# A decoder step on one core: side work issued behind the evictions of each product instead of in front of them

## The chip, the cores and the metric

The kernel runs on one core of one Trainium2 chip. The metric is the device time of one execution in microseconds (us), over three runs: median 2305.31, from 2304.89 to 2305.92. TensorE is called PE here, VectorE DVE, ScalarE ACT, GpSimd POOL; SP is the engine that issues most of the loads.

## The reference

A hybrid decoder of two layers (one of each kind), model width 2048, for 1024 prompt positions and 8 sampled positions. All is fp32.

```python
def pool_layer(x, prefix, pos, w_in, w_grp, scale, w_out, g_ln, b_ln):
    z = x @ w_in
    u, gate = z[..., :D_POOL], z[..., D_POOL:]
    d, new_state = multiscale_pool(u, prefix, pos)      # trailing means of 2, 4, 8, 16 minus u
    d = jnp.einsum('btgc,gce->btge', d.reshape(B, T, N_POOL_GROUPS, POOL_GROUP), w_grp)
    d = d.reshape(B, T, D_POOL) * scale
    y = (d * jax.nn.silu(gate)) @ w_out
    return layer_norm(ALPHA * x + y, g_ln, b_ln), new_state

def attn_layer(x, pos, kb, vb, k_pos, q_pos, blocked, w_in, sinks, w_out, g_ln, b_ln):
    z = x @ w_in
    q = rope_partial(z[..., :D_ATTN].reshape(B, T, N_HEADS, HEAD_DIM), pos)
    gate = z[..., D_ATTN:]
    o = attn_core(q, kb, vb, q_pos, k_pos, sinks)       # window of 128, grouped heads, sinks
    y = (o.reshape(B, T, D_ATTN) * jax.nn.silu(gate)) @ w_out
    return layer_norm(ALPHA * x + y, g_ln, b_ln)
```

Between the two layers one shared K and V is projected from the first layer's output. The outputs are both layers' result for prompt and sample, the pooling states and the last keys and values.

## The kernel before

**Tiles and chunks.** Activations lie with channels on the 128 partitions and positions along the free dimension. The 1032 positions are two chunks: chunk 0 with 512, chunk 1 with 520. Ten phases run one after another: `ai` (first layer's input product and pooling), `ao` (its output product), `bi` (K, V, queries, gates and the attention) and `bo` (output product), each for chunk 0 and then chunk 1; `ai0` and `bi0` are split in two.

**Products.** Almost all matrix products are Strassen-like: a pair of 128-column output tiles by 2x2 blocks takes seven products, in the order 0, 2, 1, 5, 3, 4, 6 (the function `seven`). One product is 24 matmuls (L661 to L663) into one of three PSUM banks: eight steps of high half by high half, high by low, low by high, since an fp32 operand is split in a high and a low half (fp32r) on the way. A product takes 24 times 120 ns, 2.88 us, and a pair some 20.2 us. In the first pairs of some phases two pairs run side by side.

**Weight casts.** A stream of weight blocks is loaded ahead, cast to its high half on ScalarE (L491), and the low half is the difference on VectorE (L506). `begin`, at the start of each product, issues the L506 of the product two later. The input's halves are cast likewise (L796 on ScalarE, L805 on VectorE) by `x_tick`, at the end of a product.

**Evictions.** Each product leaves a function in `self.posts`, which `flush`, called first by the next `begin`, issues: L609, L615, L618, L624 and L641 are copies on ScalarE after products 0, 1, 2, 5 and 6; L629 and L634 are subtractions on VectorE after products 3 and 4. Bank b takes products 0's negative, 1, 3 and 6, so L609, L618 and L629 must be done before the product after the next one. Behind the last eviction of a pair, in the same list, comes what is done with the pair: in `ao` and `bo` the residual addition L1287 on VectorE (ALPHA times x plus the pair, which reads what L641 copied); L1298 and L1301 add the pair to a running sum.

**Side work.** `self.side` is a list of generators, advanced by one step now and then (`self.every`) when enough slots are free: `t_gen` makes the Strassen sums of an activation (`t_ops`, L853 to L856), `sum_gen` those of a weight (L439, L443, L444, each followed by a store from POOL's queue), `ln_gen` is the norm: sums over the channels by matmuls with a constant matrix (L910), variance L1005, the reciprocal root L931 to L934, then for each of eight tile pairs minus the mean and times the root on VectorE (L1026, L1029), scale and offset on ScalarE (L1018), a store, and the next layer's sums (`t_ops`). The norm of chunk 0 runs beside the output product of chunk 1 (`ao1`, 925 to 1080 us, and `bo1`, from 2145 us); weight sums of `woa` run in `ai1`, the norm of chunk 1 in `bi0`. The sums of `wob` go through `self.extra`, which is not `self.side`.

**Order.** PE, VectorE and ScalarE run in the order of the source (`in_order` at the end makes it so). SP's and POOL's queues are ordered by the framework's scheduler. All SBUF tiles share 54 slots; a new tile gets the slot that was released longest ago, so the order of allocation decides which slot a tile lies in.

So at the border between two products the order before was: `end` of the product (events, `x_tick`, one step of side work), then `begin` of the next (`flush` with the evictions, loads, weight casts, matmuls).

Of the kernel before, what the change touches and what calls it, by code (L numbers as in the profile page):

```python
# [94 lines left out]
class Slot:  # L95


    def __init__(self, mem, i, h, a):
        self.mem, self.i, self.h, self.a = mem, i, h, a
# [83 lines left out]
class Kern:  # L183
    def __init__(self, ctx, tc, io):
        self.tc, self.io = tc, io
        self.nc = tc.nc
        pool = lambda name, **kw: ctx.enter_context(tc.tile_pool(name=name, **kw))
        one = pool("one", bufs=1)
        self.smp = pool("smp", bufs=2)
        dram = pool("dram", bufs=1, space=bass.MemoryType.DRAM)  # L190
        self.psd = [pool(f"psd{i}", bufs=1, space=bass.MemoryType.PSUM) for i in range(3)]
        self.pso = pool("pso", bufs=1, space=bass.MemoryType.PSUM)
        self.four = None
        ctx.callback(self.use_four, None)
        self.prm = one.tile([P, N_PRM], F32, name="prm")
        self.cst = one.tile([P, N_CST], F32, name="cst")
        self.mki = one.tile([P, 64], U8, name="mki")
        self.jr = one.tile([P, P], F32R, name="jr")
        area = one.tile([P, NK * NST], F32, name="area")
        three = lambda a, b, c: area[:, a : a + b * c].rearrange("p (b c) -> p b c", b=b)  # L200
        self.carry = three(0, NK, NST)
        self.kdec, self.qd, self.sgd = three(0, 2, NDEC), three(16, NDEC, 8), three(80, 8, NDEC)
        self.flag = one.tile([P, 1], F32, name="flag")
        self.mem = Mem(pool("mem", bufs=1), NSLOT)
        self.n = 0
        self.i = self.e = self.lastO = self.turns = self.ring = 0
        self.posts, self.events, self.side = [], {}, []
        self.extra, self.on = None, False
        self.fresh = None
        self.ahead = 7, 4, 3  # L210
        dr = lambda n, s: dram.tile(s, F32, tag=n, name=n)
        self.Td, self.act, self.l_sq, self.l_sh = {}, {}, {}, {}
        for c, (_, T) in enumerate(CHUNKS):
            for n, k in (("x", "ai"), ("g", "ao"), ("h", "bi"), ("o", "bo")):
                if (k, c) in STRASSEN:
                    self.Td[n, c] = dr(f"t{n}{c}", [P, 8, 4, T // 2])
            self.act["x", c] = io[f"x{c}"]
            for n in ("g", "h", "o", "p"):
                self.act[n, c] = dr(f"{n}{c}", [P, NK, T])
        self.gbd = dram.tile([32, 2 * P], F32, tag="gbd", name="gbd")  # L220
        self.ws = {
            n: [dr(f"s{n}{q}", [P, 4, 1024]) for q in range(np_)]
            for n, np_ in (("wia", 16), ("woa", 8), ("wkv", 2), ("wib", 16), ("wob", 8))
        }
# [288 lines left out]
    def flush(self):  # L513
        todo, self.posts = self.posts, []
        for go in todo:
            go()

    def begin(self):
        self.flush()
        a, b, d = self.ahead if self.strassen else (5, 4, 3)  # L520
        free = lambda: len(self.mem.whole())
        self.load_to(self.e + min(a, 5))
        while self.loaded < min(self.e + a, len(self.stream)) and free() > 2:
            self.load_to(self.loaded + 1)
        self.prep_to(self.e + (d if free() > 1 else d - 1))
        self.cast_to(self.e + (b if free() > 1 else b - 1))
        self.make_to(self.e + (b if free() > 0 else b - 1) + (1 if self.strassen else 0))
        self.e += 1
        return self.hl.pop(self.e - 1)

    def end(self):

        if self.late and self.i > 6:
            self.late.pop(0)()
        while self.i in self.pe:
            todo = sorted(self.pe.pop(self.i), key=lambda x: x[0])
            todo[0][1]()
            if todo[1:]:
                self.pe.setdefault(self.i, []).extend(todo[1:])
        for go in self.events.pop(self.i, []):  # L540
            go()
        self.i += 1
        self.x_tick()
        room = len(self.mem.whole()) - 2 * len(self.xq)
        if self.extra and next(self.extra, 1):
            self.extra = None
        if self.side and int(self.i / self.every) != int((self.i - 1) / self.every) and room >= self.room:
            if next(self.side[0], 1):
                self.side.pop(0)

    def side_step(self):
        if self.lastO >= self.i - 1:
# [706 lines left out]
    def phase_out(self, c, res, nxt, last=None):  # L1259
# [55 lines left out]
        return pre, acc  # L1315

    def shifted(self, c, p, s, pre, acc, end):

        nc = self.nc
# [1180 lines left out]
```

## Time and profile before

| | |
|---|---|
| runs shown | 2305.31 us (median of 3; 2304.89 to 2305.92) |
| profiled execution | 2305.89 us |
| its span, first to last instruction | 2304.1 us |
| granted PE clock | 0.999 of full speed |
| L506, low half of a weight, VectorE | 684 times, 1218 ns each |
| L491, high half of a weight, ScalarE | 684 times, 1048 ns each |
| L629, eviction on VectorE | 90 times, 423 ns each; VectorE idle ahead of it 74.9 us, for PE |
| L641, eviction on ScalarE | 87 times, 374 ns each; ScalarE idle ahead of it 188.5 us, for PE |
| DMA | 654.58 MB, mean 284 GB/s |

A timeline row has the start and the length in us, engine, line, operation, tile written from tiles read, shape, count, and in brackets the engine's idle time just before it and what ended that. Busy instructions of one engine overlap a little, so the next row can start before the last has ended. A PE row's length is that of a pipelined matmul; matmuls start every 0.12 us.

### The profile page before, as it was taken

To read this page: it belongs to the slowest core of one execution; us is meant where nothing else is said; L and a number is where in the kernel's file an instruction comes from. 1 tells how busy PE (TensorE), PEld (TensorE's weight loads), DVE (VectorE), ACT (ScalarE), POOL (GpSimd) and SP (SyncE) were. 2 spreads that over 40 slices of the span, in tenths; PEclk is the share of its full clock that TensorE was granted. 3 is DMA by queue.
4 is the path that set the end of the run, shared out by engine and by line. 5 is a ranking of instruction groups with operands and counts; after the bars stand their busy time and mean duration, and the time that the engine had idled before them with its cause. 6 is when DMAs were issued, how large, how long until landed. Compare 5 with 4: busy or idle time off the path is not lost. (4 is left out here: it accounts for less than half of the span.)

```text
span 2304.1 us, 50417 instructions
## 1 busy us (share of the span) xinstructions
PE 2283.5 (99%) x20279; PEld 2209.6 (96%) x20279; DVE 1902.1 (83%) x2433; ACT 1368.2 (59%) x2533; POOL 198.1 (9%) x400
## 2 busy tenths in 40 slices
PE   9999999999999999999999999999999999999998
PEld 7899999999999999999889999999999999999998
DVE  8787889777878878988888888899776777888896
ACT  4444446544546546555466776785776678656565
POOL 0111110011010000000011111100000000010001
PEclk9999999999999999999999999999999999999999
DMA  8768789988989988999687667787686678799794
GB/s 292 243 233 296 262 298 364 328 306 289 309 306 313 350 286 305 338 389 351 230 305 255 230 231 248 256 291 233 223 255 229 218 225 306 250 364 383 254 347 172
DMA packets 248220, 654.58 MB, mean 284 GB/s; under 512 B 26385, under 2 KB 106033, under 8 KB 247985
## 3 DMA queue, kind: packets, MB, share of 16 engines
q1 hardware_dynamic: 204816, 494.67, 63.8%
q0 software_dynamic: 43168, 156.68, 17.6%
q8 instruction: 159, 2.61, 0.5%
q14 instruction: 77, 0.62, 0.1%
HBM read 464.54 MB, written 177.20 MB: 279 GB/s over the span
## 5 line engine op out<-in xcount | busy, mean ns | idle before, releaser
L661 PE MATMUL pD<-m,m 128*128 128x260 f32 (+1 forms) x4976 | 1409.1, 283 | 6.8 <-DVE m L629 3.0
L662 PE MATMUL pD<-m,m 128*128 128x260 f32 (+1 forms) x4976 | 1401.8, 282 | 0.0
L663 PE MATMUL pD<-m,m 128*128 128x260 f32 (+1 forms) x4976 | 1401.2, 282 | 0.6 <-DVE m L506 0.5
L661 PEld LDWEIGHTS pD<-m,m 128*128 128x128 f32 x4976 | 936.8, 188 | 12.1 <-issue 2.3
L663 PEld LDWEIGHTS pD<-m,m 128*128 128x128 f32 x4976 | 937.3, 188 | 1.1 <-DVE m L506 1.1
L662 PEld LDWEIGHTS pD<-m,m 128*128 128x128 f32 x4976 | 936.8, 188 | 0.5
L506 DVE TENSOR_TENSOR m<-m,m 128x1024 fp32r<-128x1024 f32 x684 | 827.6, 1218 | 76.7 <-ACT m L491 42.9
L491 ACT CAST m<-m 128x1024 fp32r<-128x1024 f32 x684 | 712.8, 1048 | 286.8 <-DVE m L343 86.4
L343 DVE TENSOR_TENSOR m<-m,m 128x1024 f32<-128x1024 f32 x120 | 146.6, 1222 | 10.2 <-DMA m<-in_wia 6.9
L805 DVE TENSOR_TENSOR m<-m,m 128x1024 fp32r<-128x1024 f32 (+1 forms) x118 | 144.2, 1225 | 5.9 <-ACT m L796 3.2
L641 ACT COPY m<-pD 128x260 f32<-128x260 f32 (+1 forms) x87 | 32.5, 374 | 188.5 <-PE pD L663 188.5
L796 ACT CAST m<-m 128x1024 fp32r<-128x1024 f32 (+1 forms) x118 | 123.8, 1054 | 4.4 <-DMA m<-in_x 2.4
L689 PE MATMUL pD<-m,m 128*128 128x512 f32 x288 | 114.3, 397 | 0.0
L691 PE MATMUL pD<-m,m 128*128 128x512 f32 x288 | 113.5, 394 | 0.0
L690 PE MATMUL pD<-m,m 128*128 128x512 f32 x288 | 113.2, 393 | 0.0
L629 DVE TENSOR_TENSOR m<-pD,m 128x260 f32<-128x260 f32 (+1 forms) x90 | 38.1, 423 | 74.9 <-PE pD L663 74.9
L1870 ACT ACTIVATE m<-m,sm 128x128 f32<-128x128 f32 x256 | 99.3, 390 | 0.0
L1892 ACT ACTIVATE m<-m,sm 128x128 f32<-128x128 f32 (+1 forms) x320 | 93.8, 373 | 0.0
L1133 PE MATMUL pD<-m,m 128*128 128x260 f32 (+1 forms) x528 | 91.4, 323 | 0.0
L1133 PEld LDWEIGHTS pD<-m,m 128*128 128x128 f32 x528 | 79.4, 188 | 8.2
L618 ACT COPY m<-pD 128x260 f32<-128x260 f32 (+1 forms) x90 | 33.6, 374 | 90.3 <-PE pD L663 90.2
L609 ACT ACTIVATE pD<-pD 128x260 f32<-128x260 f32 (+1 forms) x88 | 32.5, 369 | 78.2 <-PE pD L663 68.2
(257 smaller groups left out, 2187.4 us busy)
## 6 DMA issues: line engine op xcount, KB each, us to landing
m<-in_wib SPq DMA_DIRECT2D x132, 512.0 KB
m<-in_wia SPq DMA_DIRECT2D x122, 512.0 KB
swia<-m POOLq DMA_DIRECT2D x64, 512.0 KB, 5.0
m<-swia SPq DMA_DIRECT2D x64, 512.0 KB
m<-swoa SPq DMA_DIRECT2D x64, 512.0 KB
m<-swob SPq DMA_DIRECT2D x56, 512.0 KB
m<-in_wob SPq DMA_DIRECT2D x52, 512.0 KB
m<-in_woa SPq DMA_DIRECT2D x48, 512.0 KB
```

What stands on the lines that cost most here:

```text
L343: self.nc.vector.tensor_add(s[out].a[:, :1024], s[x].a[:, :1024], s[y].a[:, :1024])
L491: self.nc.scalar.copy(hi.r[:, :1024], self.stream[self.cast].src().a[:, :1024])
L506: self.nc.vector.tensor_sub(lo.r[:, :1024], s.src().a[:, :1024], hi.a[:, :1024])
L661: nc.tensor.matmul(ps[:, :TH], wh[:, s], h, start=new and k == 0, stop=False, skip_group_check=on)
L662: nc.tensor.matmul(ps[:, :TH], wh[:, s], l, start=False, stop=False, skip_group_check=on)
L663: nc.tensor.matmul(ps[:, :TH], wl[:, s], h, start=False, stop=k == 7, skip_group_check=on)
L689: nc.tensor.matmul(ps[:], wh[:, s], h, start=par == 0 and k == 0, stop=False)
L690: nc.tensor.matmul(ps[:], wh[:, s], l, start=False, stop=False)
L691: nc.tensor.matmul(ps[:], wl[:, s], h, start=False, stop=par == 1 and k == 7)
L796: self.nc.scalar.copy(h.r[:, :n], s.a[:, :n])
L805: self.nc.vector.tensor_sub(l.r[:, :n], s.a[:, :n], h.a[:, :n])
L1133: nc.tensor.matmul(ps[:, : cs.stop - cs.start], ws[:, s], d[:, cs], start=f0 and k == 0, stop=l0 and k == 3,)
```

## The change

One step of side work that falls due in `end` is now only noted (`self.owed`), and `flush` issues it when it has issued the evictions. What else `end` does, `x_tick`'s input casts among it, stays where it was. A step that other code asks for directly (`side_step`) is issued at once, as before.

```diff
@@ Kern.__init__
-        self.posts, self.events, self.side = [], {}, []
+        self.posts, self.events, self.side, self.owed = [], {}, [], False
@@ flush
         todo, self.posts = self.posts, []
         for go in todo:
             go()
+        if self.owed and self.side:
+            self.owed = False
+            if next(self.side[0], 1):
+                self.side.pop(0)
@@ end
         if self.side and int(self.i / self.every) != int((self.i - 1) / self.every) and room >= self.room:
-            if next(self.side[0], 1):
-                self.side.pop(0)
+            self.owed = True
```

Three places show what moves. Lines behind `flush` are three or four higher in the changed kernel: L629, L634, L932, L1026, L1029, L1287 and L1301 before are L632, L637, L935, L1029, L1032, L1290 and L1304 after. Names m_.. are SBUF tiles, pD_.. PSUM banks.

VectorE in `ao1`, at 948 us, where the first full pair ends and the norm of chunk 0 has its mean and root (m_1304_10982). Before:

```order
L634 TENSOR_TENSOR m_1306_10986<-pD_10874,m_1312_11022 128x260
L506 TENSOR_TENSOR m_1343_11273<-m_1328_11135,m_1341_11244 128x1024
L1026 TENSOR_TENSOR m_1057_8981<-m_1057_8981,m_1304_10982 128x1024
L1029 TENSOR_TENSOR m_1057_8981<-m_1057_8981,m_1304_10982 128x1024
L1287 SCALAR_TENSOR_TENSOR m_1298_10945<-m_1279_10824,m_1298_10945 128x1040
L506 TENSOR_TENSOR m_1347_11310<-m_1331_11166,m_1344_11275 128x1024
```

And after:

```order
L637 TENSOR_TENSOR m_1304_10982<-pD_10874,m_1312_11022 128x260
L506 TENSOR_TENSOR m_1343_11273<-m_1328_11135,m_1341_11244 128x1024
L1290 SCALAR_TENSOR_TENSOR m_1298_10945<-m_1279_10824,m_1298_10945 128x1040
L1029 TENSOR_TENSOR m_1057_8981<-m_1057_8981,m_1305_10984 128x1024
L1032 TENSOR_TENSOR m_1057_8981<-m_1057_8981,m_1305_10984 128x1024
L506 TENSOR_TENSOR m_1347_11310<-m_1331_11166,m_1344_11275 128x1024
```

The norm's two steps have moved behind the residual addition; the weight cast stays last.

VectorE one pair later, at 970 us: the Strassen sums of a normed tile pair, the eviction of product 4, the norm of another tile pair and the residual addition. Before:

```order
L506 TENSOR_TENSOR m_1370_11521<-m_1353_11383,m_1368_11492 128x1024
L853 TENSOR_TENSOR m_1372_11549<-m_1057_8981 128x256
L854 TENSOR_TENSOR m_1372_11549<-m_1057_8981 128x256
L855 TENSOR_TENSOR m_1372_11549<-m_1057_8981,m_1372_11549 128x256
L856 TENSOR_TENSOR m_1372_11549<-m_1057_8981,m_1372_11549 128x256
L634 TENSOR_TENSOR m_1365_11486<-pD_11389,m_1357_11416 128x260
L506 TENSOR_TENSOR m_1374_11558<-m_1358_11418,m_1371_11523 128x1024
L1026 TENSOR_TENSOR m_1352_11373<-m_1352_11373,m_1304_10982 128x1024
L1029 TENSOR_TENSOR m_1352_11373<-m_1352_11373,m_1304_10982 128x1024
L1287 SCALAR_TENSOR_TENSOR m_1365_11486<-m_1356_11414,m_1365_11486 128x1040
L1301 TENSOR_TENSOR m_1278_10823<-m_1278_10823,m_1365_11486 128x1040
L506 TENSOR_TENSOR m_1379_11601<-m_1361_11449,m_1375_11560 128x1024
```

And after:

```order
L506 TENSOR_TENSOR m_1370_11521<-m_1353_11383,m_1368_11492 128x1024
L637 TENSOR_TENSOR m_1364_11479<-pD_11389,m_1357_11416 128x260
L856 TENSOR_TENSOR m_1372_11550<-m_1057_8981 128x256
L857 TENSOR_TENSOR m_1372_11550<-m_1057_8981 128x256
L858 TENSOR_TENSOR m_1372_11550<-m_1057_8981,m_1372_11550 128x256
L859 TENSOR_TENSOR m_1372_11550<-m_1057_8981,m_1372_11550 128x256
L506 TENSOR_TENSOR m_1374_11558<-m_1358_11418,m_1371_11523 128x1024
L1290 SCALAR_TENSOR_TENSOR m_1364_11479<-m_1356_11414,m_1364_11479 128x1040
L1304 TENSOR_TENSOR m_1278_10823<-m_1278_10823,m_1364_11479 128x1040
L1029 TENSOR_TENSOR m_1352_11376<-m_1352_11376,m_1305_10984 128x1024
L1032 TENSOR_TENSOR m_1352_11376<-m_1352_11376,m_1305_10984 128x1024
L506 TENSOR_TENSOR m_1379_11601<-m_1361_11449,m_1375_11560 128x1024
```

The four sums have moved behind the eviction, and the two steps of the norm behind the residual addition and the running sum.

VectorE in `bo1`, at 2174 us: the reciprocal root of the last norm of chunk 0 and the eviction of product 3. Before:

```order
L1341 TENSOR_TENSOR m_2786_26370<-m_2805_26489,m_2812_26527 128x1040
L932 TENSOR_TENSOR m_2868_26988<-m_2844_26793 128x512
L933 SCALAR_TENSOR_TENSOR m_2868_26988<-m_2868_26988 128x512
L934 SCALAR_TENSOR_TENSOR m_2844_26793<-m_2868_26988,m_2844_26793 128x512
L629 TENSOR_TENSOR m_2873_27028<-pD_26908,m_2863_26945 128x260
L506 TENSOR_TENSOR m_2878_27069<-m_2859_26911,m_2876_27034 128x1024
```

And after:

```order
L1344 TENSOR_TENSOR m_2786_26370<-m_2805_26489,m_2812_26527 128x1040
L632 TENSOR_TENSOR m_2874_27025<-pD_26903,m_2864_26946 128x260
L935 TENSOR_TENSOR m_2869_26990<-m_2844_26794 128x512
L936 SCALAR_TENSOR_TENSOR m_2869_26990<-m_2869_26990 128x512
L937 SCALAR_TENSOR_TENSOR m_2844_26794<-m_2869_26990,m_2844_26794 128x512
L506 TENSOR_TENSOR m_2879_27070<-m_2860_26912,m_2877_27035 128x1024
```

Here the eviction has moved ahead of the root's three steps.

## The prediction

> **What bounds the kernel now.** I read the page first, then the list of waits of TensorE (PE), then the busy times by stage, and last the timeline around each place where a wait and a moved row meet.
>
> ```profile
> span 2304.1 us, 50417 instructions
> ...
> PE 2283.5 (99%) x20279; PEld 2209.6 (96%) x20279; DVE 1902.1 (83%) x2433; ACT 1368.2 (59%) x2533; POOL 198.1 (9%) x400
> ```
>
> PE is idle for only 2304.1 - 2283.5 = 20.6 us. No order of the other engines can win more than this; it can lose any amount. The next view, PE's waits, shows how little of it hangs on evictions (line, what was waited for: us in all, times, longest):
>
> ```profile
> PE pD L661 <- DVE m L629: 3.0, 3, 1.3
> PE pD L661 <- ACT pD L609: 1.7, 2, 1.3
> PE pD L661 <- ACT m L618: 1.5, 1, 1.5
> ```
>
> Six waits, 6.2 us, are for an eviction (L629 on VectorE, L609 and L618 on ScalarE). I looked at each in the timeline. In five no side step stands ahead of the eviction; there it is a pooling step, a step of the attention, an input cast or, for the 1.5 us, a weight cast. One has a side step ahead of it: the 1.26 us at 2176. That is the whole direct gain.
>
> The stages decide the loss (columns: stage, its length, then busy us of PE, PEld, DVE, ACT and POOL, granted clock, DMA share, GB/s):
>
> ```profile
> 928.00:1020.00 92.00, 91.15 (x755) 90.48 (x755) 87.84 (x106) 54.68 (x76) 5.86 (x11) 1.00 0.96 353
> 2000.00:2110.00 110.00, 110.00 (x955) 109.75 (x954) 96.21 (x116) 60.14 (x80) 10.12 (x19) 1.00 0.99 361
> 2110.00:2240.00 130.00, 128.11 (x1064) 127.55 (x1063) 119.30 (x119) 82.91 (x114) 4.99 (x7) 1.00 0.89 315
> ```
>
> VectorE is busy for 87.84 of 92 us (95%) in the first of these and 119.30 of 130 (92%) in the last: there it has next to nothing to spare, and these are the stages in which the norm of chunk 0 runs as side work.
>
> **The change part by part.** No instruction is added or dropped; rows trade places. On VectorE 40 rows of 2421 change places, on ScalarE 18, on PE one (two L910 matmuls now follow an L606). Two sorts of swap have to be told apart. If the evicted product is finished when the engine gets there, it is a pure swap: the eviction comes earlier by the side step, the cast behind both stays where it was, and PE, which wasn't waiting, gains nothing. If the product is still running, the side step used to fill the wait; now the engine stands idle until the product ends, and all behind it is late by that idle time. What a cast can bear is its lead: the time from its end to the third matmul of the product that uses it (the first to read the low half, L663).
>
> *Pair A, 949 us.* VectorE, ScalarE and PE rows of the timeline:
>
> ```profile
> 949.40 1.22 DVE L1026 TENSOR_TENSOR m<-m,m 128x1024 f32<-128x1024 f32 x1
> 950.66 1.22 DVE L1029 TENSOR_TENSOR m<-m,m 128x1024 f32<-128x1024 f32 x1
> 951.80 1.23 DVE L1287 SCALAR_TENSOR_TENSOR m<-m,m 128x1040 f32<-128x1040 f32 x1
> ...
> 960.05 3.49 DVE L506 TENSOR_TENSOR m<-m,m 128x1024 fp32r<-128x1024 f32 x3
> ...
> 968.16 0.43 DVE L629 TENSOR_TENSOR m<-pD,m 128x260 f32<-128x260 f32 x1 [1.10 <-PE pD L663]
> ...
> 950.78 0.38 ACT L641 COPY m<-pD 128x260 f32<-128x260 f32 x1 [4.74 <-PE pD L663]
> ...
> 962.46 0.28 PE L663 MATMUL pD<-m,m 128*128 128x260 f32 x1
> ```
>
> The norm's L1026 and L1029 now stand behind L1287, which reads what L641 copies out. VectorE is free at 949.4, L641 ends at 950.78 + 0.38 = 951.16: 1.8 us idle, and all behind is 1.8 late. The first of the three casts at 960.05 ends 1.2 later, at 961.25; PE reads it at 962.46, so its lead is 1.2. PE waits 1.8 - 1.2 = **0.6**. The idle 1.10 ahead of L629 at 968 then takes most of the 1.2 that VectorE is behind PE's new schedule; 0.1 is left.
>
> *Pair B, 970 us.*
>
> ```profile
> 969.64 0.42 DVE L853 TENSOR_TENSOR m<-m 128x256 f32<-128x256 f32 x1
> ...
> 971.11 0.42 DVE L634 TENSOR_TENSOR m<-pD,m 128x260 f32<-128x260 f32 x1
> ...
> 974.98 1.23 DVE L1287 SCALAR_TENSOR_TENSOR m<-m,m 128x1040 f32<-128x1040 f32 x1
> 976.25 1.24 DVE L1301 TENSOR_TENSOR m<-m,m 128x1040 f32<-128x1040 f32 x1
> 977.41 1.22 DVE L506 TENSOR_TENSOR m<-m,m 128x1024 fp32r<-128x1024 f32 x1
> ...
> 970.83 0.28 PE L661 MATMUL pD<-m,m 128*128 128x260 f32 x1
> ...
> 973.89 0.38 ACT L641 COPY m<-pD 128x260 f32<-128x260 f32 x1 [3.25 <-PE pD L663]
> ...
> 979.68 0.28 PE L663 MATMUL pD<-m,m 128*128 128x260 f32 x1
> ```
>
> PE is now 0.6 late, VectorE 0.7: it is free at 970.35. L634 needs the product that ends where the row of 970.83 begins the next one, some 0.2 past that start and 0.6 late: 971.6. So 1.25 idle, and lateness about 1.95. Then L1287 waits for L641 (973.89 + 0.38 + 0.6 = 974.9), which adds some 0.3: 2.3. The cast at 977.41 ends at 978.63 + 2.3 = 980.9; PE needs it at 979.68 + 0.6 = 980.3. PE waits **0.6**, and is 1.2 late.
>
> *Pair C, 990 to 1003 us.*
>
> ```profile
> 997.64 1.22 DVE L506 TENSOR_TENSOR m<-m,m 128x1024 fp32r<-128x1024 f32 x1
> ...
> 1001.17 2.35 DVE L506 TENSOR_TENSOR m<-m,m 128x1024 fp32r<-128x1024 f32 x2
> ...
> 1028.54 0.43 DVE L629 TENSOR_TENSOR m<-pD,m 128x260 f32<-128x260 f32 x1 [2.45 <-PE pD L663]
> ...
> 999.87 0.28 PE L663 MATMUL pD<-m,m 128*128 128x260 f32 x1
> ...
> 1002.74 0.28 PE L663 MATMUL pD<-m,m 128*128 128x260 f32 x1
> ```
>
> VectorE comes 2.3 late to L634 and waits about 0.2 more (2.5 in all). The cast at 997.64 has a lead of 999.87 - 998.86 = 1.0: 2.5 - 1.2 - 1.0 = **0.3**. The next, at 1001.17, has 1002.74 - 1002.35 = 0.4: 2.5 - 1.5 - 0.4 = **0.6**. From there the leads grow, and the 2.45 idle at 1028.54 takes what is left. Sum of this stage: 0.6 + 0.6 + 0.3 + 0.6 = **+2.1 us**. Its bounds: nothing, if the leads hold; 1.8 + 1.25 + 0.3 + 0.2 = 3.6 if PE pays all the idle time.
>
> That the late work cannot be passed by what is ready behind it is what the row of 1028.54 shows: VectorE sat 2.45 us at an eviction with a cast queued behind. The Trainium skill, TensorE: Matmul & The Clock Gate, table at the top, says the same as a rule: VectorE and ScalarE have queues of 8 in strict first-in, first-out order. The trace agrees, with that 2.45 us. Were the rule not to hold, this stage would cost nothing, and only the gain below would stand.
>
> *The reciprocal root at 2174 us.*
>
> ```profile
> 2174.41 0.69 DVE L933 SCALAR_TENSOR_TENSOR m<-m 128x512 f32<-128x512 f32 x1
> 2175.13 0.69 DVE L934 SCALAR_TENSOR_TENSOR m<-m,m 128x512 f32<-128x512 f32 x1
> 2175.74 0.42 DVE L629 TENSOR_TENSOR m<-pD,m 128x260 f32<-128x260 f32 x1
> ...
> 2195.81 0.41 DVE L629 TENSOR_TENSOR m<-pD,m 128x260 f32<-128x260 f32 x1
> ...
> 2176.31 0.36 PE L661 MATMUL pD<-m,m 128*128 128x260 f32 x1 [1.26 <-DVE m L629]
> ...
> 2196.57 0.28 PE L661 MATMUL pD<-m,m 128*128 128x260 f32 x1
> ```
>
> L629 moves ahead of L932 to L934, which take over 2 us, so PE's 1.26 goes. But the next L629, at 2195.81, ends at 2196.22, only 0.35 before PE needs it, and VectorE has no idle time between the two, so it isn't earlier. PE gets there 1.26 earlier and waits 0.9. Net **-0.35 us**; bounds -1.26 (all kept) and 0.
>
> *The rest.* ScalarE's swaps are mostly affine steps (L1018) behind evictions; it is busy for 54.68 of 92 us, which hides them, and a cast behind is delayed by two L1018 at most. SP's loads (39 rows) and POOL's (6) also trade places, because these two queues are ordered by the scheduler, and side steps take their buffers after the evictions, so that from there on tiles lie in other slots. Their cost is unknown. No row of PE's waits names a load; the nearest row is L618's 1.5 us, where a cast on ScalarE had waited for a slot that VectorE freed late. I bound it by one such wait gone and two more of them, -1.5 to +3.0, and take 0, since slots are still dealt by age.
>
> Sum: 2.1 - 0.35 = +1.75. The profiled execution took 2305.89 us (span 2304.1 and 1.8 around it); with the change 2307.6. The median is 0.6 below that execution, so **2307.1 us**, 0.08% up, which is less than the 0.2% (4.6 us) that a measurement of this kernel can tell from no change.
>
> **The rivals.** *Faster:* the leads hold, as the waits at L634 and L1287 are shorter than I read them, and the 1.26 stays won: 2305.3 - 1.3 = 2304.0. For it: every eviction that moves comes no later. Against it: VectorE's 95%. The Trainium skill, PSUM — Partial Sum Buffer, summary for kernel authors, advises to evacuate promptly; this rival is what that would give here, and the trace bears it out at one eviction only, the 1.26 us above.
>
> *Slower:* at 2034 to 2160 the same turn happens, and the leads there fail.
>
> ```profile
> 2035.98 1.23 DVE L1287 SCALAR_TENSOR_TENSOR m<-m,m 128x1024 f32<-128x1024 f32 x1 [0.20 <-ACT m L641]
> ...
> 2049.79 0.42 DVE L629 TENSOR_TENSOR m<-pD,m 128x256 f32<-128x256 f32 x1 [2.02 <-PE pD L663]
> ```
>
> Transposition sums (L853 to L856, four in 1.6 us) stood ahead of L1287 at 2035.98, and filled all but 0.20 of its wait; now some 1.7 are idle. Two more pairs (2052 and 2150) lose about 1.3 each: 4.3 in all. I hide them behind idle time such as the 2.02 at 2049.79. But the DMA engines are 99% busy here: a cast that ends late frees its slot late, the load into it starts late and can't catch up. From the point where a load comes later than the lead of its cast, PE pays all three: 2307.1 + 4.3 = 2311.4. Against it: the idle rows, and no PE wait for a load.
>
> *Nothing happens:* nearly all swaps are pure, as products are done when VectorE gets there, and 2176 is won only to be lost at 2196: 2305.3.
>
> **How the numbers follow.** Forecast 0.5, faster 0.2, slower 0.2, nothing 0.1. Low: 2304.0 and one wait of 1.5 less, 2302.5. High: the slower rival, 2311.4, which also holds the upper bounds of the forecast (2307.1 + 1.5 + 3.0 = 2311.6, about the same). Beyond 0.2%: above 2309.9 lies the slower rival, 0.2; below 2300.7 only several slot waits gone at once, 0.03; the rest, 0.77, is the same.
>
> **What would show it.** In the profile after: PE's row of 1.26 at 2176 gone, with a new wait for L629 some 20 us later; new PE waits for L506 of 0.3 to 0.7 each between 958 and 1003; rows of L634 and L1287 there with an idle time [.. <-PE] or [.. <-ACT m L641] of 1 to 2 us where before there was none. I am wrong if PE has no wait for L506 in that stage, or if the new waits lie in the attention stage (1270 to 2000), which would be the slots.

## The result and the profile after

| | before | after |
|---|---|---|
| median of 16 runs each, us | 2305.80 (2304.16 to 2307.47) | 2309.92 (2306.64 to 2314.58) |
| ratio of times | | 1.0018, 95% interval 1.0012 to 1.0025 |
| profiled execution, us (its span) | 2305.89 (2304.1) | 2309.18 (2307.4) |

The change costs 4.1 us (by the interval 2.8 to 5.8). The 2309.92 us lie inside the forecast range, 2.8 us above the forecast itself; 0.5 of that is the kernel before, which stands at 2305.80 here and stood at 2305.31. The forecast rise of 1.8 us lies below the interval, and by the time alone the rival *slower* (2311.4) came nearer: only the profile decides between the two. The lines in the changed kernel stand three or four higher (L506 is the same). The engines' busy times on its page, and TensorE's waits (line, what it waited for: us in all, times, longest):

```profile
PE 2285.8 (99%) x20279; PEld 2210.8 (96%) x20279; DVE 1902.4 (82%) x2433; ACT 1367.7 (59%) x2533; POOL 198.9 (9%) x400
```

```profile
PE pD L666 <- DVE m L506: 2.7, 5, 1.1
PE pD L664 <- DVE m L632: 2.1, 3, 0.9
PE pD L664 <- ACT pD L612: 1.8, 2, 1.3
PE pS L1832 <- DVE m L1798: 1.8, 2, 0.9
PE pD L664 <- ACT m L621: 1.5, 1, 1.5
```

Of the 6.2 us of waits for an eviction, 5.4 are left (L632, L612, L621). At the top now stands L506, the cast of a weight. Before, it had one wait:

```profile
PE pD L663 <- DVE m L506: 0.5, 1, 0.5
```

That wait, at 929, is still among the five and takes 1.1 us in this execution (the ledger's column 930 below); the other four are new. The stages whose VectorE share the prediction quoted:

```profile
928.00:1020.00 92.00, 89.02 (x726) 87.56 (x726) 85.55 (x101) 52.92 (x73) 5.87 (x11) 1.00 0.95 345
2000.00:2110.00 110.00, 110.00 (x974) 109.61 (x974) 95.46 (x119) 59.07 (x79) 10.70 (x20) 1.00 0.99 356
2110.00:2240.00 130.00, 129.15 (x1076) 128.80 (x1075) 120.62 (x120) 82.72 (x114) 4.99 (x7) 1.00 0.89 310
```

In the first, PE is busy 2.1 us less than before in the same 92 us. The second still has no idle time. VectorE's timeline of the first stage shows why:

```profile
951.39 1.24 DVE L1290 SCALAR_TENSOR_TENSOR m<-m,m 128x1040 f32<-128x1040 f32 x1 [1.07 <-ACT m L644]
952.55 1.22 DVE L1029 TENSOR_TENSOR m<-m,m 128x1024 f32<-128x1024 f32 x1
953.81 1.23 DVE L1032 TENSOR_TENSOR m<-m,m 128x1024 f32<-128x1024 f32 x1
...
962.04 3.49 DVE L506 TENSOR_TENSOR m<-m,m 128x1024 fp32r<-128x1024 f32 x3
...
972.04 0.43 DVE L637 TENSOR_TENSOR m<-pD,m 128x260 f32<-128x260 f32 x1 [1.31 <-PE pD L666]
972.38 0.41 DVE L856 TENSOR_TENSOR m<-m 128x256 f32<-128x256 f32 x1
...
975.30 1.24 DVE L1290 SCALAR_TENSOR_TENSOR m<-m,m 128x1040 f32<-128x1040 f32 x1 [0.23 <-ACT m L644]
...
993.00 0.43 DVE L637 TENSOR_TENSOR m<-pD,m 128x260 f32<-128x260 f32 x1 [0.31 <-PE pD L666]
...
963.32 0.39 PE L666 MATMUL pD<-m,m 128*128 128x260 f32 x1 [0.39 <-DVE m L506]
981.40 0.39 PE L666 MATMUL pD<-m,m 128*128 128x260 f32 x1 [0.57 <-DVE m L506]
1002.03 0.39 PE L666 MATMUL pD<-m,m 128*128 128x260 f32 x1 [0.20 <-DVE m L506]
1005.57 0.39 PE L666 MATMUL pD<-m,m 128*128 128x260 f32 x1 [0.37 <-DVE m L506]
```

VectorE now stands idle ahead of each eviction or residual addition that has come first (the brackets), the side step that used to fill that time follows, and some products later PE waits for the cast behind both.

**A ledger of PE's schedule.** PE runs the same 20279 matmuls in every trace here, so the start of the k-th one can be compared between two traces. Where the difference jumps, time was lost or won. Below are the jumps against the profiled execution of before, in us; times are those of before. A, B and C are the prediction's pairs (950 to 965, 965 to 985, 985 to 1010). Bold are those places whose order the kernel changes.

| kernel | A | B | C | 1173 | 1262 | 2176 | 2196 | 930 | 1240 | 1690 | 2131 |
|---|---|---|---|---|---|---|---|---|---|---|---|
| after | **0.78** | **0.85** | **1.18** | **0.83** | **0.53** | **-1.55** | **1.07** | 0.80 | -0.14 | 0.01 | -0.87 |
| ao1_only | **0.76** | **0.79** | **1.17** | -0.01 | -0.01 | -0.04 | 0.03 | 0.41 | 0.88 | -0.15 | -0.82 |
| all_but_ao1 | 0.01 | 0.04 | 0.04 | **0.01** | **0.46** | **-1.44** | **1.15** | 0.70 | 0.63 | 0.21 | -0.51 |
| bi_only | 0.00 | 0.00 | 0.00 | **1.70** | **0.45** | -0.09 | 0.03 | 0.33 | -0.31 | 1.35 | -0.84 |
| bo1_only | 0.00 | 0.00 | 0.00 | 0.00 | 0.01 | **-1.47** | **1.11** | 0.55 | 0.01 | 1.55 | -0.89 |
| residual_last | **0.00** | **0.46** | **1.13** | -0.03 | -0.01 | -0.04 | 0.04 | 0.35 | -0.32 | -0.32 | -0.85 |
| relief_before | 0.00 | 0.00 | 0.00 | 0.00 | -0.01 | -0.01 | 0.00 | 0.97 | -0.15 | 0.74 | -0.91 |
| relief_ao1 | **0.74** | **-0.01** | **0.03** | -0.01 | 0.00 | -0.04 | 0.03 | 0.21 | 0.00 | 0.59 | 0.09 |
| bo1_square | 0.00 | 0.00 | 0.00 | 0.00 | 0.01 | **-1.49** | **1.04** | 0.13 | 0.01 | 0.78 | 0.40 |
| bo1_relief | 0.00 | 0.00 | 0.35 | 0.00 | 0.00 | **-1.49** | **-0.02** | 0.26 | -0.31 | 0.63 | -0.55 |

bo1_only issues everything up to 1923 us exactly as before, and still its trace differs at 930 by 0.55 and at 1690 by 1.55. So the four columns on the right are chance between two executions, up to 1.5 us at one place. The columns on the left repeat to about 0.1 us where a kernel shares the changed order, except 1173 (and but for 0.35 at C in bo1_relief, which changes nothing there). One trace's end says little here; one place's jump says much.

### The profile page after: what moved, and what is told of

It reads as the page before. It is cut to its first block, busy times and chain, and to the rows that moved or that the text cites. A ratio compares the mean times of both kernels' runs of the same rounds, so it can differ in the third digit from the quotient of the medians.

```text
span 2307.4 us, 50405 instructions
## 1 busy us (share of the span) xinstructions
PE 2285.8 (99%) x20279; PEld 2210.8 (96%) x20279; DVE 1902.4 (82%) x2433; ACT 1367.7 (59%) x2533; POOL 198.9 (9%) x400
## 5 line engine op out<-in xcount | busy, mean ns | idle before, releaser
L506 DVE TENSOR_TENSOR m<-m,m 128x1024 fp32r<-128x1024 f32 x684 | 828.1, 1219 | 75.8 <-ACT m L491 41.9
L632 DVE TENSOR_TENSOR m<-pD,m 128x260 f32<-128x260 f32 (+1 forms) x90 | 38.2, 424 | 82.0 <-PE pD L666 81.8
L621 ACT COPY m<-pD 128x260 f32<-128x260 f32 (+1 forms) x90 | 33.7, 375 | 93.0 <-PE pD L666 92.7
L612 ACT ACTIVATE pD<-pD 128x260 f32<-128x260 f32 (+1 forms) x88 | 32.5, 369 | 78.3 <-PE pD L666 64.9
```

Source lines behind the costliest of these rows:

```text
L506: self.nc.vector.tensor_sub(lo.r[:, :1024], s.src().a[:, :1024], hi.a[:, :1024])
```

## The experiments

Most variants are after with a condition on the phase in `end`; it is the whole diff of the first four, with its own phases in each:

```diff
         if self.side and int(self.i / self.every) != int((self.i - 1) / self.every) and room >= self.room:
-            self.owed = True
+            if self.ph == "ao1":
+                self.owed = True
+            elif next(self.side[0], 1):
+                self.side.pop(0)
```

Lines of these kernels are six above those of before (L635 is L629, L640 is L634, L647 is L641, L667 to L669 are the matmuls).

**1. Only in `ao1`.**

> Side steps stand behind the evictions only in the output product of the first layer, chunk 1 (about 911 to 1075 us), and ahead of them as before everywhere else. Theory (VectorE has nothing to spare there, so its idle time in front of evictions makes casts late): TensorE falls back by 2.8 us between 955 and 1005 us (1.8 to 3.5), in waits for L506, and the whole kernel is 2 to 3.5 us slower than before, about as slow as the full change. Rival (the loss comes from tiles in other slots and later loads): under 1 us is lost in this stretch, and what is lost comes after 1080 us, in waits behind a load.

Measured: 1.0018 (1.0009 to 1.0027), median 2309.66 against 2305.78. In the ledger 2.72 us are lost between 950 and 1010, 2.6 of them at the four waits for L506. In the medians this stage alone makes the time of the whole change.

**2. Everywhere else** (`self.ph != "ao1"`).

> The other half of the pair: side steps stand behind the evictions everywhere but in that output product. Theory: nothing is lost between 955 and 1005 us; what is left is the sum of the small steps elsewhere, between -0.5 and +1.5 us against before. Rival (slots and loads): +2.5 to +4 us, as with the full change, most of it after 1080 us.

Measured: 1.0003 (0.9994 to 1.0011), median 2306.65. Nothing is lost between 950 and 1010 (0.09 in all). What remains at changed places is 0.46 - 1.44 + 1.15 = +0.2 us. The rival, slots dealt anew and late loads, asked for 2.5 us or more, and falls as the main cause.

**3. Only in `bi0` and `bi1`** (`self.ph in ("bi0", "bi1")`).

> Side steps stand behind the evictions only in the input products of the second layer (1075 to 1790 us). The full change lost 0.9 us at 1173 and 0.5 us at 1263 us there. If the rows moved within this stage cause that, the same +1.0 to +1.4 us shows up at the same two places, with the 7.1 us wait of SP's queue for a tile that is still being stored. If it comes from slots dealt in the stage before, nothing is lost here: 0.0, within 0.3 us.

Measured: 1.0005 (0.9996 to 1.0014). Both steps are there, so they come from rows moved within this stage. PE, VectorE and the waits of SP's queue (between 1120 and 1180) in bi_only:

```profile
1174.88 1.53 PE L1835 MATMUL pS<-m,m 64*64 64x192 f32 x32 [1.59 <-DVE m L1801]
1263.89 1.53 PE L1835 MATMUL pS<-m,m 64*64 64x192 f32 x32 [0.94 <-DVE m L1801]
...
1172.71 1.30 DVE L1694 TENSOR_TENSOR m<-m,m 128x512 f32<-128x512 f32 x2 [2.40 <-DMA m<-m]
```

```profile
SPq L792 <- DMA th<-m: 6.6, 1, 6.6
```

SP's queue stands 6.6 us (7.1 in after, 1.7 in before, each time behind a store to `th`) at a load whose slot is still being stored; the load that L1694 needs comes late, and VectorE waits 2.40 for it. all_but_ao1 has the same order and the same wait of SP (6.5), but its VectorE waits 1.79 and PE nothing: at 1173 the moved rows only make a loss possible, 0 to 1.7 us. How SP's wait gets to PE isn't shown: in ao1_only, with the order of before here, SP waits 1.6, VectorE still 1.78 at this row, and PE nothing. At 1262 the wait is 0.94 in all three kernels with this order, against 0.49 before; what lengthens it is open.

**4. Only in `bo1`** (`self.ph == "bo1"`).

> Side steps stand behind the evictions only in the last output product (from 1923 us). Theory (the wait of 1.26 us at 2176 goes, and 0.9 to 1.1 us of it come back at the next L629, at 2196, since VectorE has no idle time between): -0.4 us net there. Rival (all of it is kept): -1.3 us. If the 0.9 us that the full change won at 2131 comes from this stage too, a further -0.9 us; if it came from slots dealt earlier, none.

Measured: 1.0004 (0.9995 to 1.0013). PE's wait at 2176 is gone (-1.47), and this one is new:

```profile
2196.88 0.36 PE L667 MATMUL pD<-m,m 128*128 128x260 f32 x1 [0.84 <-DVE m L635]
```

1.11 comes back there: net -0.36, the prediction's -0.35. The 0.9 at 2131 is chance, since it is as large in kernels that change nothing there.

**5. Evictions ahead, the residual addition behind the side step**, in `ao1` only. `flush` issues the step behind the first function in its list, so that L641 goes ahead and L1287 doesn't:

```diff
-        for go in todo:
-            go()
-        if self.owed and self.side:
-            self.owed = False
-            if next(self.side[0], 1):
-                self.side.pop(0)
+        for n, go in enumerate(todo + [lambda: None]):
+            if n == min(1, len(todo)) and self.owed and self.side:
+                self.owed = False
+                if next(self.side[0], 1):
+                    self.side.pop(0)
+            go()
```

> As ao1_only, but a pair's residual addition (L1287) stays behind the side step; only the eviction itself goes ahead of it. Theory (the loss is VectorE's idle time ahead of a product or a copy that isn't finished): the 1.8 us in front of L1287 in pair A are filled again, so the 0.67 us at 962 goes; pair B keeps its idle 1.25 at L634 and pays 0.3 instead of 0.84, pair C 0.6 to 0.7 in all. So 0.9 to 1.3 us in place of 2.7 between 955 and 1005. Rival (what makes the casts late is the cast's place behind the side step, wherever the idle time is): all four steps stay, 2.5 us or more.

Measured: 1.0008 (0.9999 to 1.0018); in the ledger 0.00, 0.46 and 1.13, together 1.59: more than the theory's 0.9 to 1.3, well under the rival's 2.5. VectorE's and PE's rows:

```profile
971.21 0.43 DVE L640 TENSOR_TENSOR m<-pD,m 128x260 f32<-128x260 f32 x1 [1.30 <-PE pD L669]
991.82 0.43 DVE L640 TENSOR_TENSOR m<-pD,m 128x260 f32<-128x260 f32 x1 [0.29 <-PE pD L669]
...
980.25 0.39 PE L669 MATMUL pD<-m,m 128*128 128x260 f32 x1 [0.23 <-DVE m L506]
1000.86 0.39 PE L669 MATMUL pD<-m,m 128*128 128x260 f32 x1 [0.21 <-DVE m L506]
1004.39 0.39 PE L669 MATMUL pD<-m,m 128*128 128x260 f32 x1 [0.39 <-DVE m L506]
```

In pair A, where VectorE's order is that of before again, the idle time and the loss go together; experiment 7 separates the idle time from the order. Pair C was expected at 0.6 to 0.7 and kept its 1.13, although VectorE now came earlier to pair B. The wait of 1.30 at L640 is as long as in after (1.31): once VectorE waits for a product, its rows behind run by PE's clock, and what it gained or lost before is wiped out.

**6 and 7. Giving VectorE slack.** In both, for pairs 2 to 7:

```diff
-                else:
+                elif self.ph != "ao1":
                     nc.vector.tensor_add(flat(acc), flat(acc), flat(s))
```

> The kernel before, with the running sum of the pairs (L1301, 1.24 us of VectorE per pair) left out for pairs 2 to 7 of the first layer's output product, chunk 1, so that the norm of chunk 1 gets a partial sum. It gives VectorE 7.4 us of slack in 164 us. It is the base for relief_ao1. Both theories: TensorE hardly waited there, so the time stays within 0.6 us of before's.

> ao1_only with the same sums (L1301) left out. Theory (a full VectorE can't make good the idle time before the cast is due): with 1.24 us more of lead per pair the idle times of 1.2 to 1.8 us are covered, and the stage loses 0.0 to 0.8 us against relief_before in place of 2.7. Rival (an eviction's place costs this whatever VectorE has to spare): the four steps of 0.5 to 0.8 us stay, 2.4 to 2.8 in all.

Measured: 0.9999 (0.9990 to 1.0009) and 1.0008 (0.9998 to 1.0017). Against relief_before, in the ledger, B and C lose nothing (-0.01 and 0.03) in place of 0.79 and 1.17. A loses its 0.74 as before: it lies at 963, and the first sum that is left out would come at 976, so VectorE has no more slack there. VectorE's and PE's rows of relief_ao1:

```profile
950.91 1.25 DVE L1293 SCALAR_TENSOR_TENSOR m<-m,m 128x1040 f32<-128x1040 f32 x1 [1.04 <-ACT m L647]
971.49 0.43 DVE L640 TENSOR_TENSOR m<-pD,m 128x260 f32<-128x260 f32 x1 [1.30 <-PE pD L669]
991.62 0.43 DVE L640 TENSOR_TENSOR m<-pD,m 128x260 f32<-128x260 f32 x1 [0.77 <-PE pD L669]
...
962.84 0.39 PE L669 MATMUL pD<-m,m 128*128 128x260 f32 x1 [0.41 <-DVE m L506]
```

The same 1.30 us of idle time at 971 costs PE 0.8 us where VectorE is full and nothing where it has 1.24 us to spare; at 992 it is even longer (0.77) and free. An idle time costs only what the next cast's lead doesn't cover. The medians say less: relief_ao1 (2307.66) lies 2.3 us above relief_before (2305.36), which is more than the ledger's 0.74; with an interval of about 2 us on either side of each, this neither shows nor excludes a further loss.

**8. The square of the root on ScalarE**, with `bo1` only:

```diff
-        nc.vector.tensor_mul(q, r, r)
+        if self.ph == "bo1":
+            nc.scalar.activation(q, r, AF.Square)
+        else:
+            nc.vector.tensor_mul(q, r, r)
```

> bo1_only with the first operation of the reciprocal root's refinement (the square of the root, L932, 0.69 us on VectorE) done on ScalarE in that stage. If the 1.1 us that came back at 2196 are VectorE's lack of time between 2176 and 2196, 0.7 of them stay won: -1.5 at 2176, +0.4 at 2196, net -1.1 us instead of -0.4. If something else holds the L629 of 2196 (the product, ScalarE), the +1.1 stays. In the median it is at most 0.05%, and that can't be told from no change.

Measured: 0.9997 (0.9988 to 1.0007); -1.49 and +1.04. This looks like the rival, but VectorE's row shows that the variant freed hardly any of VectorE's time:

```profile
2175.49 0.69 DVE L942 SCALAR_TENSOR_TENSOR m<-m 128x512 f32<-128x512 f32 x1 [0.53 <-ACT m L939]
```

VectorE waits 0.53 us for the square, so of 0.69 us only some 0.1 to 0.2 were won, and the return shrank by 0.07.

**9 and 10. The running sum of squares on GpSimd**, on before and on `bo1` only:

```diff
-            nc.vector.tensor_add(flat(self.l_sq[c]), flat(self.l_sq[c]), flat(box["q"]))
+            add = nc.gpsimd.tensor_add if self.ph == "bo1" and p < 6 else nc.vector.tensor_add
+            add(flat(self.l_sq[c]), flat(self.l_sq[c]), flat(box["q"]))
```

> The kernel before with one addition per pair of the last output product (L1350, the running sum of squares, 1.23 us on VectorE, six pairs) done on GpSimd, which is idle there (4.99 of 130 us busy). It is the base for bo1_pool. The wait of 1.26 us at 2176 stays, as the root still stands ahead of the eviction; at 2196 VectorE has 2.5 us more. Time within 0.6 us of before's, unless GpSimd's additions slow VectorE's own rows.

> bo1_only with the same additions on GpSimd. Two of them (L1350 at 2177.2 and 2192.4) lie between the won wait at 2176 and the lost one at 2196. bo1_square gave VectorE back only 0.1 us there (it waited 0.53 us for ScalarE's square) and so couldn't settle this. Theory (the return at 2196 is VectorE's lack of time): 2.5 us more cover the 1.1 us, so -1.5 at 2176 and 0.0 to +0.2 at 2196, a net of -1.3 against -0.4 in bo1_only. Rival (another cause holds that L629): the +1.1 stays. In the median that is 0.06%, inside what can't be told from no change.

Measured: 1.0028 (1.0018 to 1.0038) and 1.0030 (1.0018 to 1.0042), the one proviso in the expectation come true. Nothing can be read of the return at 2196: the wait at 2176 isn't won either (1.13 at 2179), since VectorE is held up just ahead of it. The profiled execution of bo1_pool is its longest (2320.55 against a median of 2312.74). Rows of VectorE and GpSimd in it:

```profile
2175.43 3.48 DVE L1347 TENSOR_TENSOR m<-m,m 128x1040 f32<-128x1040 f32 x1
2198.97 3.13 DVE L506 TENSOR_TENSOR m<-m,m 128x1024 fp32r<-128x1024 f32 x1
...
2174.98 2.83 POOL L1357 TENSOR_TENSOR m<-m,m 128x1040 f32<-128x1040 f32 x1 [3.15 <-ACT m L1342]
2189.80 11.22 POOL L1357 TENSOR_TENSOR m<-m,m 128x1040 f32<-128x1040 f32 x1
```

And the group of GpSimd's additions (count, us in all, mean ns; idle time ahead):

```profile
L1357 POOL TENSOR_TENSOR m<-m,m 128x1040 f32<-128x1040 f32 x4 | 26.5, 6634 | 7.4 <-ACT m L1342 7.2
```

There are four of them, not the six of the expectation: only pairs 1 to 4 take this way in the last phase.

**11. Leaving the sum out instead**, for pairs 1 to 4, with `bo1` only:

```diff
-            nc.vector.tensor_add(flat(self.l_sq[c]), flat(self.l_sq[c]), flat(box["q"]))
+            if self.ph != "bo1" or p >= 6:
+                nc.vector.tensor_add(flat(self.l_sq[c]), flat(self.l_sq[c]), flat(box["q"]))
```

> bo1_only with the running sum of squares (L1350) left out for pairs 1 to 4 of the last output product, so that the variance of chunk 1 comes from a partial sum. bo1_pool couldn't settle the return at 2196, because VectorE's own rows grew beside GpSimd's additions. Here the same 2.5 us of VectorE go between 2176 and 2196 without work elsewhere. Theory (VectorE's lack of time): -1.5 us at 2176, 0.0 to +0.2 at 2196. Rival (another cause): +1.1 at 2196 as in bo1_only.

Measured: 1.0001 (0.9992 to 1.0010); -1.49 at 2176 and -0.02 at 2196. The return is gone. VectorE, which stood late at that eviction, now has time over at the next:

```profile
2194.45 0.42 DVE L635 TENSOR_TENSOR m<-pD,m 128x260 f32<-128x260 f32 x1
...
2196.50 0.43 DVE L640 TENSOR_TENSOR m<-pD,m 128x260 f32<-128x260 f32 x1 [0.50 <-PE pD L669]
```

So VectorE's lack of time is enough to explain the return; no other cause is needed.

**12. The sum later instead of left out**, an attempt at a version that keeps the 1.1 us:

```diff
-                self.at(1, more)
+                self.at(6 if self.ph == "bo1" else 1, more)
```

> bo1_only, but L1350 comes six products after its pair's other additions in place of one, so that one of the two additions between 2176 and 2196 lies behind the second place; nothing is left out. Theory: 1.2 us of room cover most of the 1.1: -1.5 at 2176 and 0.0 to +0.4 at 2196, net -1.1 to -1.5 in the trace, if the debt of 1.2 us doesn't reach TensorE at a later eviction, which would give the 1.1 back there. Against it: a square's buffer is held 15 us longer, so a load may come later. In the median that is at most 0.06%, inside what can't be told from no change.

Measured: 1.0013 (1.0004 to 1.0023), 3.7 us more than before, a miss. Something was changed that the expectation overlooked: the additions of chunk 0's last two pairs fall in this phase too, and come after the norm has taken their sum, so that its variance leaves them out. VectorE and PE:

```profile
2152.13 1.28 DVE L890 TENSOR_TENSOR m<-m 128x512 f32<-128x512 f32 x2
2157.35 1.22 DVE L1356 TENSOR_TENSOR m<-m,m 128x1024 f32<-128x1024 f32 x1
...
2163.72 1.22 DVE L1356 TENSOR_TENSOR m<-m,m 128x1024 f32<-128x1024 f32 x1
...
2179.21 0.36 PE L667 MATMUL pD<-m,m 128*128 128x260 f32 x1 [1.19 <-DVE m L635]
```

L890 sums the squares at 2152, the two late additions follow at 2157 and 2164, and take VectorE's time just ahead of the root: the wait at 2176 is there again (1.19), and PE loses 1.0 at 2171 and 0.8 at 2196 besides. It tells nothing for or against the theory, only that VectorE's debt can't be put off by moving it to another full stretch. No variant beats before by more than a measurement can tell.

## Why the prediction held, point by point

- **VectorE sets the price, not the evictions.** Right. One stage (`ao1`) carries the loss: ao1_only gives the full change's time, all_but_ao1 nearly none of it.
- **Idle times.** Forecast 1.8 us before L1287 in pair A, 1.25 and 0.3 in pair B, 0.2 in pair C; measured 1.07, 1.31, 0.23 and 0.31. The 1.07 is shorter because VectorE came to it late already, by a swap that the prediction overlooked. Before, steps of the norm stood ahead of the evictions at 942 and 946 (variance and root); now VectorE idles at both. Before and after:

```profile
942.80 0.42 DVE L629 TENSOR_TENSOR m<-pD,m 128x260 f32<-128x260 f32 x1
946.32 0.42 DVE L634 TENSOR_TENSOR m<-pD,m 128x260 f32<-128x260 f32 x1
948.27 1.22 DVE L506 TENSOR_TENSOR m<-m,m 128x1024 fp32r<-128x1024 f32 x1
```

```profile
941.88 0.43 DVE L632 TENSOR_TENSOR m<-pD,m 128x260 f32<-128x260 f32 x1 [1.32 <-PE pD L666]
945.23 0.43 DVE L637 TENSOR_TENSOR m<-pD,m 128x260 f32<-128x260 f32 x1 [0.40 <-PE pD L666]
949.10 1.22 DVE L506 TENSOR_TENSOR m<-m,m 128x1024 fp32r<-128x1024 f32 x1
```

  The last cast ahead of pair A starts 0.83 later, 0.66 without PE's own shift of 0.17. With the 1.07 that makes 1.7, about the forecast 1.8: the sum was right, its place in part not. It isn't chance, since ao1_only and relief_ao1 have 1.04 at this row. The casts behind start at 962.04, 1.99 later than before, 1.8 without the shift.
- **The term that was too small: the PE waits.** 0.6, 0.6 and 0.3 + 0.6 were forecast (2.1), 0.78, 0.85 and 1.18 measured (2.81). Against the matmul just ahead of them, the four that wait start 0.55, 0.74, 0.36 and 0.53 later than before, together 2.2, so in sum the waits themselves were sized well. The rest lies beside them. Behind each, the next matmul follows after 0.22 us in place of 0.12 (0.4 in all). And in pair A one matmul, at 959.79, started 0.11 late behind a cast that ended at 958.51 + 1.22 = 959.73, without a wait in the profile. Some 0.1 is spread thinly.
- **Lateness from pair to pair.** Once VectorE waits for a product, its lateness is set anew, so each pair has its own price. The prediction's sum allows for this, as its 2.5 in pair C stands behind such a wait; its upper bound of 3.6, which adds up all idle times, and the expectation of residual_last for pair C (0.6 to 0.7, measured 1.13) don't.
- **The root:** forecast -0.35, measured -0.48 in after, -0.36 in bo1_only, and bo1_relief bears out the reason that was given, no idle time between the two evictions.
- **The rest, taken at 0** (-1.5 to +3.0): the second term that was too small. At 1262 the changed order costs 0.5 us in every trace, at 1173 it cost 0.8 in this execution and 0.0 and 1.7 in two others. Both lie in `bi0`, not in the attention stage that the prediction would have put slots in. At 1173 SP's queue waits for a slot, which is the mechanism that was left unpriced; how it gets to PE is open, as is the cause at 1262.
- **The rivals.** *Faster* fails at VectorE's lack of time, as its counter-argument had it. *Slower* (2034 to 2160) doesn't happen, although its time came nearer: PE has no idle time from 2000 to 2110, and in the ledger nothing is lost at 2150 either.
- **The range.** It held, but it was 8.9 us wide for a change of 4.1, and its upper end came from a rival that didn't happen. That the measured time lies inside says little; the waits for L506 and the step at 2176 say more.

In sum, at changed places, 2.81 + 0.83 + 0.53 - 1.55 + 1.07 = 3.7 us, against a measured 2.8 to 5.8. The rest of the 4.1 can't be told from chance. Part of the wider spread of the runs after (8 us, against 3.3 before) goes with the granted PE clock, which is 0.998 in the three longest (2312.04, 2313.82 and 2314.58) and 0.999 in the other thirteen, up to 2311.19. Whether the change has a part in that isn't shown: before itself spread over 5.6 us beside the first four experiments, and bo1_only, without the costly stage, over 5.7.

## What to carry to other kernels

A side step in front of an eviction isn't lost time if the product isn't finished yet: it fills a wait that the engine would have anyway. Before changing the order, look at whether the eviction's source is done when the engine gets there, and how much lead the next work on that engine has; in a full stage put the eviction first only where PE is really waiting for it. And a wait that is removed on a full engine has to be followed to the next place where that engine is late, as here 20 us on.

## What the hardware showed besides

**VectorE and GpSimd stop each other.** In bo1_pool four additions of 128x1040 took 26.5 us on GpSimd (mean 6.6), while rows of VectorE that take 1.2 us elsewhere took up to 3.48. The Trainium skill, SBUF — State Buffer, section on the two separate sides, says that the two share a pair of ports which one of them locks for a whole instruction, also for a VectorE operation with two inputs in SBUF against a GpSimd one that reads there. The stretched rows agree; the 11.22 us, through the first 9 of which VectorE's rows kept their 1.2 us, show that GpSimd can be kept out for many instructions.

**A long wait of PE was followed by a slower clock.** Moving four times 1.23 us of work to an engine that was idle cost 6.7 us in pool_before (2312.71 against 2306.01). In its trace PE loses 3.45 us at 2176 and 4.12 at 2246 (times of before, as in the ledger). Two rows of PE, and the stretch around the first (columns as in the prediction, the clock after POOL):

```profile
2178.49 0.36 PE L661 MATMUL pD<-m,m 128*128 128x260 f32 x1 [3.22 <-DVE m L629]
2251.65 0.59 PE L661 MATMUL pD<-m,m 128*128 128x260 f32 x1 [2.38 <-ACT m L618]
```

```profile
2165.00:2185.00 20.00, 16.78 (x126) 16.52 (x126) 17.05 (x17) 10.58 (x14) 3.38 (x2) 0.91 0.66 220
```

The clock is 0.91 on average here, and 1.00 in the same stretch before: within 2 us after each wait matmuls start every 0.22 us in place of 0.12, for some 3 us. That is 1.5 us of each loss, 3 of 7.6 us, so not all of the price is the two engines' conflict. The second wait is for ScalarE, which had itself waited 4.78 us for a load; how that hangs together with GpSimd, and that the wait is what slows the clock, isn't shown further.

**A short wait of PE costs more than the list of waits shows.** The four brackets of `ao1` add up to 0.39 + 0.57 + 0.20 + 0.37 = 1.53 us, but PE loses 2.6 at these four places. The idle time is counted from the modelled end of a matmul of 0.28 us that would have been followed after 0.12, so 0.16 of each stop doesn't show, and the matmul behind the waiting one comes 0.10 later than usual. The Trainium skill, Perfetto Trace Analysis, section on the Tensor Engine instruction, says that TensorE's end times are computed from the instruction's size and not observed. This case agrees: the time lost is read from the starts of matmuls, not from the waits.
